# A hybrid recurrence and attention layer on one core: the second of four norm sums of a recurrence unit stands one stage of the mixer later

## The chip, the cores and the metric

The kernel runs on one core of one Trainium2 chip, as one program. The metric is the device time of one execution in microseconds (us). Before the change three runs took 2640.05, 2636.79 and 2634.97 us: a median of 2636.79 us. TensorE is called PE here, VectorE DVE, ScalarE ACT; SP issues the DMA transfers, and its queue is strictly in order.

## The reference, cut to what matters

The layer projects a normalised input (2048 tokens, 1024 channels) into nine groups of columns, runs a bidirectional gated linear recurrence over five of them and a neighbourhood attention over the other four, multiplies each branch by its gate, and projects back. The change concerns the end of the recurrence branch, for each of 8 heads:

```python
o = direction(zf_fw, lb_fw, False) + direction(zf_bw, lb_bw, True)
o = _rmsnorm(o.transpose(0, 2, 1, 3), norm_g).reshape(B, S, HG_WIDTH)
return o.astype(g_in.dtype) * jax.nn.silu(g_in)

def _rmsnorm(x, g):
    xf = x.astype(jnp.float32)
    return xf * lax.rsqrt(jnp.mean(jnp.square(xf), axis=-1, keepdims=True) + RMS_EPS) * g.astype(jnp.float32)
```

`direction` walks the tokens in chunks and carries a state from chunk to chunk, forwards once and backwards once. The mean of squares is taken over the 128 channels of a head.

## The kernel before, in words

**Phases.** The tokens are worked in two halves of 1024. A first phase holds the projections and the attention of the first half. Then comes the recurrence phase that the change touches: 16 units, one for each head and half (the loop at the end of the block below: `half, u = divmod(i, 8)`). Two more phases hold the attention of the second half and the output projection.

**What fills a unit.** `weave` interleaves two generators. The *dense* one is the projection of the next unit: groups of three 128x512 matmuls (`proj_mm`, L278; in the last unit of the phase also `vproj`, L291), which keep PE busy while the other engines work. The *mixer* is `hgrn`: for each of two groups of 512 tokens six pieces, each ended by a `yield` of a number; the pieces are called stages 0 to 5 (first group) and 6 to 11 (second group) here. The numbers, 5, 5, 3, 3, 6 and 5, say how much dense work follows each stage. So 3 units of dense work (stages 2 and 3, and 8 and 9) are the short stretches, 6 (stages 4 and 10) the long ones.

**The tail.** The outputs of a unit are finished in the next one, by a third generator, `hgrn_tail`; each stage of the mixer takes one step of it (`next(tail, None)`), 12 steps at most, before the rest of the stage's own work. In the second half (7 units with a tail in the mixer, and one tail at the end of the phase) a tail finishes four blocks of 512 tokens, and each ends in `rms_out`, with a norm sum: the two matmuls of L350 and L351, which sum the squares over the partitions.

- first output: group 1 of the second half. Stage 0 computes its backward states, stage 1 adds them on PE (L643), copies the output out of PSUM (L645) and squares it (L343 on ACT), then splits the square into a rounded part `rh` (L345 on DVE) and a rest `rl` (L347). Stage 2 holds its norm sum, the logarithm and exponential (L353, L354 on ACT), two multiplies on DVE (L355, L357) and the store to `yq` (L358).
- second output: group 0 of the second half, in the same way: L643 to L347 in stage 3, norm sum and what follows in stage 4, and with it the loads of `cl` (L661 to L663) for the third output.
- third and fourth output: the two groups of the first half, kept in DRAM since. Stage 5 multiplies the final backward state by a stored factor (`pc<-cl`, L666, two instructions on PE), adds the stored output (L667 on DVE), squares and splits; stage 6 holds the sum of the third. Stages 7 and 8 do the same for the fourth.

**What sets the order.** On PE the program order of the code is kept (`manual_schedule`). On ACT, DVE and SP a scheduler orders the instructions when the program is built, by priorities and its own estimates; on the chip each engine then runs its list strictly in order. Buffers: the tag `t` (output copy, square, rate, finished output) has 2, `cl` has 3, `rh` and `rl` have 1 each, and the PSUM tag `po`, in which `ss` and `pc` live too, has 2.

Of the kernel before, what the change touches and what calls it, by code (L numbers as in the profile page):

```python
# [21 lines left out]
HALF = 1024  # L22
# [16 lines left out]
def body(ctx: ExitStack, tc: tile.TileContext, t):  # L39
# [13 lines left out]
    @contextmanager  # L53
    def psum_phase(name, psb, pmap={}):
        with tc.tile_pool(name="p" + name, bufs=1, space=PSUM, reuse_waits="tile") as q:
            cur.update(psum=q, ps=psb, map=pmap)
            yield

    @contextmanager
    def phase(name, bufs, smap={}):  # L60
        with tc.tile_pool(name=name, bufs=1, reuse_waits="tile") as p:
            cur.update(pool=p, bufs=bufs, smap=smap)
            yield
# [24 lines left out]
    def nm(s):  # L88
        cnt[0] += 1
        return f"{s}_{cnt[0]}"  # L90

    def tl(tag, dt=F32, shape=None):
        if tag in cur["smap"]:
            tag = cur["smap"][tag]
            return sh.tile([P, 512], dt, tag=tag, name=nm(tag), bufs=SH[tag])
        return cur["pool"].tile([P, 512] if shape is None else shape, dt, tag=tag, name=nm(tag), bufs=cur["bufs"].get(tag, 1))
# [4 lines left out]
    def ps(tag="mx"):  # L101
        if tag == "pj":
            return pp.tile([P, 512], F32, tag=tag, name=nm("pj"))
        tag = cur["map"].get(tag, tag)
        return cur["psum"].tile([P, 512], F32, tag=tag, name=nm("ps"), bufs=cur["ps"][tag])
# [219 lines left out]
    def hgrn_init():  # L325
        p = cur["pool"]
        msk["mskd"] = p.tile([P, 3, 32], F32, tag="mskd", name="mskd")
        dma(msk["mskd"], t["mskd"])
        for i in range(2):
            b = p.tile([P, 2 * P], F32, tag=f"pdb{i}", name=f"pdb{i}")  # L330
            pool.memset(b, 0.0)
            pdb.append(b)
        for u in range(NHEAD):
            sfb.append(p.tile([P, P], F32, tag=f"sfb{u}", name=f"sfb{u}"))
# [3 lines left out]
        act.activation(e, e, AF.Ln, bias=1.0)  # L338
        act.activation(e, e, AF.Exp, scale=-1.0)

    def rms_out(u, g, o_sb, sg, tok):
        sq = tl("t")
        act.activation(sq, o_sb, AF.Square)  # L343
        sh_ = tl("rh", F32R)
        dve.tensor_copy(sh_, sq)  # L345
        sl_ = tl("rl", F32R)
        dve.tensor_tensor(sl_, sq, sh_, op=ALU.subtract)  # L347
        yield
        pss = ps("ss")
        pe.matmul(pss, ones, sh_, start=True, stop=False)  # L350
        pe.matmul(pss, ones, sl_, start=False, stop=True)  # L351
        r = tl("t")
        act.activation(r, pss, AF.Ln, scale=1.0 / 128.0, bias=eps_rms)  # L353
        act.activation(r, r, AF.Exp, scale=-0.5)  # L354
        dve.tensor_mul(r, r, o_sb)  # L355
        yv = tl("t")
        dve.tensor_tensor(yv, r, sg, op=ALU.mult)  # L357
        dma(yT[u][:, tok:tok + 512], yv)  # L358
# [60 lines left out]
    def hgrn(u, half, st, tail):  # L419
# [191 lines left out]
        for _ in tail:  # L611
            pass
        return hgrn_tail(u, half, sgs, ubs, decs, qibs, os_, decb_all)

    HSUM = 54

    def hgrn_tail(u, half, sgs, ubs, decs, qibs, os_, decb_all):

        R = None
        if half == 0:  # L620
            ds_ = tl("dsuf", shape=[P, 8])
            pool.memset(ds_[:, 7:8], 1.0)
            for b in range(6, -1, -1):
                dve.tensor_mul(ds_[:, b:b + 1], ds_[:, b + 1:b + 2], decb_all[:, b + 1:b + 2])
        obs = {}
        for g in (1, 0):
            po = os_[g]
            pend = []
            for b in range(3, -1, -1):
                sl = slice(b * P, (b + 1) * P)  # L630
                if R is not None:
                    pend.append((sl, R))
                if half == 0 and g == 0 and b == 0:
                    break
                rn = tl("Sb", shape=[P, P])
                if R is None:
                    dve.tensor_copy(rn, ubs[g][:, sl])
                else:
                    dve.scalar_tensor_tensor(rn, R, decs[1, g][:, b:b + 1], ubs[g][:, sl], op0=ALU.mult, op1=ALU.add)
                R = rn  # L640
            yield
            for sl, r in pend:
                pe.matmul(po[:, sl], r, qibs[1, g][:, sl], start=False, stop=True, skip_group_check=True)  # L643
            ob = tl("t")
            act.activation(ob, po, AF.Copy)  # L645
            tk = slice(g * 512, (g + 1) * 512)
            if half == 0:
                dma(op_d[u][:, tk], ob)
                dma(sg_d[u][:, tk], sgs[g])
                qb = tl("t")  # L650
                for b in range(4):
                    sl = slice(b * P, (b + 1) * P)
                    dve.tensor_scalar(qb[:, sl], qibs[1, g][:, sl], ds_[:, g * 4 + b:g * 4 + b + 1], 1.0, op0=ALU.mult, op1=ALU.mult)
                dma(qb_d[u][:, tk], qb)
            else:
                yield from rms_out(u, g, ob, sgs[g], HALF + g * 512)
        if half == 1:
            for g in range(2):
                tk = slice(g * 512, (g + 1) * 512)
                qb, o1, sg = tl("cl"), tl("cl"), tl("cl")  # L660
                dma(qb, qb_d[u][:, tk])  # L661
                dma(o1, op_d[u][:, tk])
                dma(sg, sg_d[u][:, tk])  # L663
                yield
                po = ps("pc")
                pe.matmul(po, R, qb, start=True, stop=True)  # L666
                dve.tensor_tensor(o1, po, o1, op=ALU.add)  # L667
                yield from rms_out(u, g, o1, sg, g * 512)
# [234 lines left out]
    def vstream(*pairs):  # L903
        for p2 in pairs:
            for _ in vproj(t["w_v"][p2], nv_d[p2], 1):
                yield 2.9
# [429 lines left out]
    def border_dense(dense):  # L1336
        yield from vstream(0)
        yield from dense
        yield from vstream(1)

    BTOT = NLEN + 2 * VLEN
# [8 lines left out]
    def weave(mix, dense, total, steps, last=0, ahead=0.0):  # L1350

        got, done, cum = [], [0.0], 0.0

        def upto(x):
            while done[0] < x and not got:
                try:
                    done[0] += next(dense)
                except StopIteration as e:
                    got.append(e.value)

        share = HTOT / total if last else 1.0
        upto(ahead)
        while True:
            try:
                cum += next(mix)
            except StopIteration as e:
                tail = e.value
                break
            upto(ahead + (total * share - ahead) * cum / steps)
        if last:  # L1370
            for i, _ in enumerate(tail):
                upto(total * (share + (1 - share) * (i + 1) / last))
        upto(1e9)
        return tail, got[0]

    h_alloc()
    with psum_phase("n0", NPS), tc.manual_schedule(engines={mybir.EngineType.PE}):
        with phase("st", SB_, SMS), tc.manual_schedule(engines={getattr(mybir.EngineType, e) for e in ("PE", "SP", "Activation", "DVE")}):
            raws, feed = startup()
        with phase("n0", NB0, SM0):  # L1380
            natten_init(4, 0)
            st = first_half(raws, feed)
# [7 lines left out]
    with psum_phase("h", *HPS), phase("h", HB, SMH), tc.manual_schedule(engines={mybir.EngineType.PE}):  # L1390
        hgrn_init()
        tail = iter(())
        for i in range(16):
            half, u = divmod(i, 8)
            if i < 15:
                nxt = hgrn_dense((i + 1) % 8, (i + 1) // 8, i in (6, 7), reload if i == 6 else None)
                tail, st = weave(hgrn(u, half, st, tail), nxt, HTOT, HSUM)
            else:
                raws, dense = natten_stream(0, 1)
                st0 = Prep(0, 1, raws)  # L1400
                for n in ("q", "k0", "k1", "g"):
                    st0.fetch(n)
                for c in (0, 1):
                    st0.v(c, "V0")
                weave(hgrn(u, half, st, tail), border_dense(dense), BTOT, HSUM, 9)

    wo, parts = {}, {}

# [122 lines left out]
    with psum_phase("n1", NPS), phase("n1", NB1, SM1), tc.manual_schedule(engines={mybir.EngineType.PE}):  # L1531
        natten_init(4, 1)
        st = st0
# [9 lines left out]
        for u in range(8):  # L1543
            nxt, extra = None, None
            if u < 7:
                raws, dense = natten_stream(u + 1, 1, feed, u + 1 == 7)
                total = NLEN
                if u == 0:
                    dense, total = chain(vs, dense), NLEN + 1.375 * VLEN
# [4 lines left out]
            else:  # L1554
                y_split(0, 1)
                dense, total = out_stream(list(range(NE))), NE * 16 * KUS
                extra = {0: [(wo_split, 0, 6, 7), (wo_load, 1, 2, 3)], 1: [(wo_split, 1, 0, 1), (wo_load, 1, 6, 7)], 2: [(wo_split, 1, 2, 3, 4, 5)], 3: [(wo_split, 1, 6, 7)]}
            weave(natten_woven(st, nxt, pipe, extra), dense, total, 24)
            st = nxt
# [77 lines left out]
```

## Time and profile before

| what | value |
|---|---|
| runs | 2634.97 to 2640.05 us, median 2636.79 us |
| the profiled execution's own time | 2634.39 us |
| its span, first to last instruction | 2632.5 us |
| PE busy in matmuls | 2564.7 us (97%) |
| DVE, ACT busy | 1736.9 us (66%), 1430.8 us (54%) |
| mean granted clock of PE | 0.992 |
| stretch with the seven second-half tails in the mixer | 1180 to 1702 us |
| one such unit, from first norm sum to first norm sum (1191.56 to 1267.23 us) | 75.7 us |

Times in the profile are counted from the first instruction. A row of the timeline gives the start, the length, the engine, the line of the kernel, the operation, `out<-in` by tile names, the shapes, and how many instructions are merged in the row; in square brackets stands how long the engine had sat idle, and who ended that. A busy PE is one with a matmul in flight: consecutive 128x512 matmuls start 0.23 us apart but last 0.4 us each, so a small wait shows as a longer distance between starts before it shows as idle time.

### The profile page before, as it was taken

How to read it: one execution, taken by the hardware profiler on the slowest of the kernel's cores; microseconds unless marked ns; L12 is line 12 of the kernel's file. 1: busy time of each engine (PE TensorE's matmuls, PEld its weight loads, DVE VectorE, ACT ScalarE, POOL GpSimd, SP SyncE). 2: the span in 40 equal slices, each digit the busy share in tenths (PEclk: the TensorE clock that was granted, in tenths of full speed). 3: DMA queues.
4: the chain of work that ended last, by engine and by line, in shares of the span. 5: the costliest groups of instructions: out<-in, count | busy, mean ns of one | idle time of the engine just before them, and what ended most of it. 6: DMA issues, size and time to landing. Idle time of an engine off the chain costs nothing.

```text
span 2632.5 us, 45805 instructions
## 1 busy us (share of the span) xinstructions
PE 2564.7 (97%) x17140; PEld 2150.0 (82%) x17140; DVE 1736.9 (66%) x4354; ACT 1430.8 (54%) x2856; POOL 108.7 (4%) x143
## 2 busy tenths in 40 slices
PE   6999999989999999999999999999999998999998
PEld 5888888878888888888888888888888887788887
DVE  7444545377777778877787777555777778548443
ACT  4534444366666666666666666454677777431110
POOL 0000000000000000000000000000000000042221
PEclk9999999999999999999999999999999999999999
DMA  7466454212111126212221222344455556443331
GB/s 271 140 212 143 132 174 152 94 46 69 65 65 58 64 73 220 84 46 77 77 65 57 72 74 73 107 120 146 126 139 140 142 142 173 125 154 128 96 96 57
DMA packets 225631, 295.87 MB, mean 112 GB/s; under 512 B 28807, under 2 KB 117511, under 8 KB 224263
## 3 DMA queue, kind: packets, MB, share of 16 engines
q1 hardware_dynamic: 225407, 292.93, 36.4%
q8 instruction: 135, 2.21, 0.4%
q14 instruction: 89, 0.73, 0.1%
HBM read 217.65 MB, written 66.99 MB: 108 GB/s over the span
## 4 chain that ended last, share of the span: by engine, by line
PE 73%; DVE 3%; ACT 2%; DMA 1%; issue 0%; DVEq 0%; ACTq 0%
PE pj L278 39%; PE ps L1466 4%; PE ps L1467 4%; PE ps L1468 4%; PE pj L291 3%; PE ps L1098 3%; PE ps L1076 2%; PE ps L478 2%; PE ps L470 1%; PE ps L545 1%; PE ps L1027 1%; PE ps L569 1%; PE ps L517 1%; PE ps L571 1%; PE ps L643 1%; DMA yq<-t 1%
## 5 line engine op out<-in xcount | busy, mean ns | idle before, releaser
L278 PE MATMUL pj<-h,wh 128*128 128x512 f32 x4000 | 1272.7, 399 | 4.2 <-ACT wh L815 1.9
L278 PEld LDWEIGHTS pj<-h,wh 128*128 128x128 f32 x4000 | 724.9, 188 | 156.3 <-issue 13.9
L278 PE MATMUL pj<-h,wl 128*128 128x512 f32 x2000 | 783.5, 392 | 0.0
L278 PEld LDWEIGHTS pj<-h,wl 128*128 128x128 f32 x2000 | 375.4, 188 | 82.9 <-DVE wl L791 0.4
L1048 ACT ACTIVATE pbuf<-pbuf,mx 128x480 f32<-128x480 f32 (+5 forms) x256 | 152.4, 597 | 114.0 <-DVE mx L1043 113.2
L291 PE MATMUL pj<-wh,h 128*128 128x256 f32 x1024 | 198.8, 289 | 4.1 <-ACT vt L297 3.8
L1043 DVE CUSTOM_DVE_ANT_1 pbuf<-ps,bias 128x480 f32<-128x480 f32 (+5 forms) x256 | 129.1, 540 | 105.1 <-PE ps L1034 47.1
L291 PEld LDWEIGHTS pj<-wh,h 128*128 128x128 f32 x1024 | 165.5, 194 | 7.9 <-ACT vt L297 4.5
L268 ACT ACTIVATE wh<-wr 128x512 fp32r<-128x512 f32 x192 | 120.2, 626 | 81.6 <-PE pj L278 72.3
L269 DVE TENSOR_TENSOR wl<-wr,wh 128x512 fp32r<-128x512 f32 x192 | 131.6, 685 | 46.7 <-ACT wh L268 45.8
L291 PE MATMUL pj<-wl,h 128*128 128x256 f32 x512 | 146.1, 285 | 0.0
L1082 ACT ACTIVATE pt<-ps 120x384 f32<-120x384 f32 (+3 forms) x128 | 65.2, 509 | 117.8 <-PE ps L1076 117.5
L464 DVE TENSOR_TENSOR de<-e,de 128x512 f32<-128x512 f32 x64 | 44.3, 692 | 117.6 <-ACT de L463 117.6
L1080 DVE COPY pt<-ps 120x384 f32<-120x384 f32 (+3 forms) x128 | 75.0, 586 | 65.3 <-PE ps L1076 64.1
L1076 PE MATMUL ps<-ident,pbuf 128*128 128x128 f32 (+2 forms) x832 | 113.3, 274 | 1.7 <-DVE pbuf L1053 1.3
L1076 PEld LDWEIGHTS ps<-ident,pbuf 128*128 128x128 f32 (+2 forms) x832 | 97.2, 137 | 19.3 <-ACT pbuf L1048 1.7
L764 ACT ACTIVATE e<-pj 128x512 f32<-128x512 f32 x98 | 58.3, 595 | 86.6 <-PE pj L278 79.6
L1442 ACT ACTIVATE yh<-yr 128x512 fp32r<-128x512 f32 x52 | 32.7, 628 | 132.4 <-PE ps L1467 115.2
L1053 DVE TENSOR_SCALAR pbuf<-pbuf,mx 128x480 f32<-128x480 f32 (+5 forms) x256 | 101.2, 413 | 3.9
L1515 DVE TENSOR_TENSOR vt<-ps,gt 128x512 f32<-128x512 f32 x24 | 16.5, 691 | 130.6 <-PE ps L1468 130.6
L291 PEld LDWEIGHTS pj<-wl,h 128*128 128x128 f32 x512 | 99.5, 194 | 1.4 <-issue 0.5
L445 DVE TENSOR_TENSOR_SCAN c<-c,g 128x128 f32<-128x128 f32 x256 | 88.4, 405 | 10.7 <-ACT c L435 10.7
(274 smaller groups left out, 4684.9 us busy)
## 6 DMA issues: line engine op xcount, KB each, us to landing
wr<-in_w_in SPq DMA_DIRECT2D x276, 256.0 KB
yr<-yq SPq DMA_DIRECT2D x64, 256.0 KB
bias<-tint SPq DMA_DIRECT2D x24, 480.0 KB
x<-in_x SPq DMA_DIRECT2D x32, 256.0 KB
ada<-in_ada_m SPq DMA_DIRECT2D x8, 1024.0 KB
wr<-in_w_v SPq DMA_DIRECT2D x32, 256.0 KB
nv<-vt SPq DMA_DIRECT2D x32, 256.0 KB
hs<-s SPq DMA_DIRECT2D x32, 256.0 KB
```

Source lines behind the costliest of these rows:

```text
L268: act.activation(hi, raw, AF.Copy)
L269: dve.tensor_tensor(lo, raw, hi, op=ALU.subtract)
L278: pe.matmul(pz, a, b, start=(k == 0 and n == 0), stop=(k == KT - 1 and n == 2))
L291: pe.matmul(pzs[tp][:, i * 256:(i + 1) * 256], a, b, start=(k == 0 and n == 0 and i == 0), stop=(k == KT - 1 and n == 2), skip_group_check ...
L445: dve.tensor_tensor_scan(c[:, sl], c[:, sl], L[:, sl], 0.0, op0=ALU.add, op1=ALU.subtract)
L1043: return dve.tensor_tensor_reduce(s[:, 0:nk].rearrange("p (r c) -> p r c", c=kw), sc[:, 0:nk].rearrange("p (r c) -> p r c", c=kw), bt[:, 0 ...
L1048: act.activation(s[:, 0:nk], s[:, 0:nk], AF.Exp, scale=-1.0, bias=mx[:, 0:1], accum_out=mx[:, 1:2])
L1053: dve.tensor_scalar(s[:, 0:nk], s[:, 0:nk], mx[:, 2:3], 1.0, op0=ALU.mult, op1=ALU.mult)
L1076: pe.transpose(ptp[0:cw, c * P:(c + 1) * P], s[:, c * cw:(c + 1) * cw], ident)
L1466: pe.matmul(pz, yh[:, kk], wh, start=first, stop=False)
L1467: pe.matmul(pz, yh[:, kk], wl, start=False, stop=False)
L1468: pe.matmul(pz, yl[:, kk], wh, start=False, stop=last)
```

## The change

The generator `rms_out` gets a flag; with it, it yields once more between the split of the square and the norm sum. The second output (group 0 of the second half) passes the flag. So its norm sum moves from stage 4 to stage 5, and everything behind it in the tail moves one stage: the third output's product from stage 5 to 6 and its sum from 6 to 7, the fourth's from 7 and 8 to 8 and 9. The tail now takes 10 steps of the 12. The last tail, which runs against the value projection, is told 10 steps in place of 9; there PE's order comes out as before. No instruction is added or removed.

```diff
-    def rms_out(u, g, o_sb, sg, tok):
+    def rms_out(u, g, o_sb, sg, tok, rest=False):
...
         dve.tensor_tensor(sl_, sq, sh_, op=ALU.subtract)
         yield
+        if rest:
+            yield
         pss = ps("ss")
...
-                yield from rms_out(u, g, ob, sgs[g], HALF + g * 512)
+                yield from rms_out(u, g, ob, sgs[g], HALF + g * 512, g == 0)
...
-                weave(hgrn(u, half, st, tail), border_dense(dense), BTOT, HSUM, 9)
+                weave(hgrn(u, half, st, tail), border_dense(dense), BTOT, HSUM, 10)
```

In the changed kernel the lines behind the new yield are two higher: the sums of L350 and L351 are L352 and L353, the product of L666 is L668, and so on.

Place 1: PE in stages 4 and 5 of the first unit concerned (numbers behind the names are buffers; between the rows left out stand dense matmuls). Before:

```order
L470 MATMUL ps_12610<-ident,de_12540 128x128 x4
...
L350 MATMUL ps_12631<-rh_12593,ones 128x512
L351 MATMUL ps_12631<-rl_12595,ones 128x512
L478 MATMUL ps_12647<-v_12390,ke_12615 128x128 x4
...
L666 MATMUL ps_12752<-cl_12641,Sb_12524 128x512
L545 MATMUL ps_12761<-x_12687,x_12688 64x64 x8
```

The same place on PE now:

```order
L472 MATMUL ps_12610<-ident,de_12540 128x128 x4
...
L480 MATMUL ps_12631<-v_12390,ke_12615 128x128 x4
...
L352 MATMUL ps_12736<-rh_12593,ones 128x512
L353 MATMUL ps_12736<-rl_12595,ones 128x512
L547 MATMUL ps_12752<-x_12671,x_12672 64x64 x8
```

The second sum (`rh_12593`, `rl_12595`) has left its place behind 12 dense matmuls and ahead of the state updates (L478, now L480), and stands where the third output's product stood, 27 dense matmuls further on.

Place 2: stages 8 and 9 of the same unit, PE first and then ACT. Before, on PE, from stage 7 on:

```order
L666 MATMUL ps_12881<-cl_12840,Sb_12524 128x512
...
L350 MATMUL ps_12948<-rh_12886,ones 128x512
L351 MATMUL ps_12948<-rl_12888,ones 128x512
L470 MATMUL ps_12958<-ident,de_12908 128x128 x4
...
L478 MATMUL ps_13005<-v_12828,ke_12963 128x128 x4
```

The same place on PE now:

```order
L668 MATMUL ps_12939<-cl_12875,Sb_12524 128x512
L472 MATMUL ps_12948<-ident,de_12899 128x128 x4
...
L352 MATMUL ps_12995<-rh_12944,ones 128x512
L353 MATMUL ps_12995<-rl_12946,ones 128x512
L480 MATMUL ps_13005<-v_12819,ke_12953 128x128 x4
```

On ACT before, there:

```order
L343 ACTIVATE t_12884<-cl_12841 128x512
L353 ACTIVATE t_12951<-ps_12948,eps_rms 128x512
L472 ACTIVATE ke_12963<-ps_12958 128x512
L463 ACTIVATE de_13310<-c_13233 128x128 x4
L354 ACTIVATE t_12951<-t_12951 128x512
```

And on ACT now:

```order
L474 ACTIVATE ke_12953<-ps_12948 128x512
L465 ACTIVATE de_13310<-c_13233 128x128 x4
L343 ACTIVATE t_12942<-cl_12876 128x512
L387 ACTIVATE vt_12980<-pj_12917 128x512
L268 ACTIVATE wh_13244<-wr_13242 128x512
L355 ACTIVATE t_12998<-ps_12995,eps_rms 128x512
```

The fourth output's product (L668) now opens stage 8, and its sum (`rh_12944`, `rl_12946`) opens stage 9, behind four transposes (L472) and 15 dense matmuls; on ACT its square (L343) stands behind the copy of the transposes and four exponentials.

Place 3: DVE in the seventh unit (the last of the phase) between the second output's split and the mask of the scores (`pm`, which PE waits for in stage 6). Before:

```order
L347 TENSOR_TENSOR rl_17656<-t_17652,rh_17654 128x512
L269 TENSOR_TENSOR wl_17878<-wr_17875,wh_17877 128x512
L355 TENSOR_TENSOR t_17705<-t_17705,t_17650 128x512
L555 COPY_PREDICATED pdb_5315<-mskd,ps_17725 128x128
L357 TENSOR_TENSOR t_17709<-t_17705,sg_16463 128x512
...
L667 TENSOR_TENSOR cl_17713<-ps_17834,cl_17713 128x512
...
L345 CAST rh_17839<-t_17837 128x512
L558 TENSOR_TENSOR pm_17860<-pdb_5315 32x4x32 x4
```

The same place now:

```order
L347 TENSOR_TENSOR rl_17656<-t_17652,rh_17654 128x512
L269 TENSOR_TENSOR wl_17869<-wr_17866,wh_17868 128x512
L557 COPY_PREDICATED pdb_5315<-mskd,ps_17709 128x128
...
L560 TENSOR_TENSOR pm_17851<-pdb_5315 32x4x32 x4
L357 TENSOR_TENSOR t_17821<-t_17821,t_17650 128x512
```

The second output's two multiplies, the third output's addition (L667) and its rounding (L345) no longer stand ahead of the mask.

On SP the second output's store moves behind two loads of weights, and two further loads of weights move ahead of the fourth output's `cl<-op`; the count of transfers is the same.

## The prediction

> **What bounds the kernel now.** I read the page first, then PE's waits in the stretch of the change, then PE's rows around the norm sums. The page has the span and PE's share:
>
> ```profile
> span 2632.5 us, 45805 instructions
> PE 2564.7 (97%) x17140; PEld 2150.0 (82%) x17140; DVE 1736.9 (66%) x4354; ACT 1430.8 (54%) x2856; POOL 108.7 (4%) x143
> ```
>
> PE is the bound, so only what PE waits for, or runs slowly, can be won. PE's waits from 1180 to 1640 us, the first six of the seven units concerned (in total, times, longest):
>
> ```profile
> PE ps L350 <- DVE rh L345: 2.6, 6, 0.6
> PE ps L351 <- DVE rl L347: 1.4, 6, 0.2
> ```
>
> Six waits each: one of four norm sums per unit. The rows of PE in the first unit say which, and show a sum that does not wait (1231.45); then stand the sums of the sixth unit and of the seventh:
>
> ```profile
> 1200.68 0.39 PE L278 MATMUL pj<-h,wl 128*128 128x512 f32 x1
> 1201.58 0.49 PE L350 MATMUL ps<-rh,ones 128*128 128x512 f32 x1 [0.51 <-DVE rh L345]
> 1202.31 0.50 PE L351 MATMUL ps<-rl,ones 128*128 128x512 f32 x1 [0.23 <-DVE rl L347]
> 1231.22 0.40 PE L278 MATMUL pj<-h,wl 128*128 128x512 f32 x1
> 1231.45 0.40 PE L350 MATMUL ps<-rh,ones 128*128 128x512 f32 x1
> 1231.92 0.60 PE L470 MATMUL ps<-ident,de 128*128 128x128 f32 x4
> 1579.47 0.49 PE L350 MATMUL ps<-rh,ones 128*128 128x512 f32 x1 [0.41 <-DVE rh L345]
> 1580.20 0.50 PE L351 MATMUL ps<-rl,ones 128*128 128x512 f32 x1 [0.23 <-DVE rl L347]
> 1655.11 0.28 PE L291 MATMUL pj<-wh,h 128*128 128x256 f32 x1
> 1658.73 0.49 PE L350 MATMUL ps<-rh,ones 128*128 128x512 f32 x1 [3.35 <-DVE rh L345]
> 1659.46 0.50 PE L351 MATMUL ps<-rl,ones 128*128 128x512 f32 x1 [0.23 <-DVE rl L347]
> ```
>
> It is the second sum, the one the change moves. Start to start it costs more than its idle time: 0.90 us from 1200.68 to 1201.58 where 0.23 is the rule (1231.22 to 1231.45), and 0.73 to L351 where an unhindered pair takes 0.47 together. That is 0.67 + 0.49 = 1.16 us in the first unit and 0.08 to 0.10 less in the sixth, by its idle time; over the six, whose idle times before L350 are 0.43 on average (2.6 / 6) against 0.51 here, 1.08 each, or 6.5. In the seventh it is 3.62 - 0.12 = 3.5, and 0.5: 4.0.
>
> The long wait has a second price. The same work, state updates and diagonal blocks, in the first unit and behind the long wait (busy times of PE, PEld, DVE, ACT, POOL with counts, PEclk, DMA share, GB/s):
>
> ```profile
> 1202.64:1204.46 1.82, 1.82 (x73) 1.65 (x71) 0.00 (x0) 1.82 (x4) 0.00 (x0) 1.00 0.00 0
> 1659.80:1662.83 3.03, 3.03 (x73) 2.74 (x71) 0.90 (x2) 1.91 (x3) 0.00 (x0) 0.54 0.29 87
> 1662.83:1664.50 1.67, 1.67 (x19) 1.67 (x12) 1.53 (x4) 0.00 (x0) 0.00 (x0) 0.81 0.05 10
> ```
>
> At a granted clock of 0.54 it took 1.21 us more; the next 1.67 us, at 0.81, lost 0.19 x 1.67 = 0.3. Together 1.5. The Trainium skill ("TensorE: Matmul & The Clock Gate", Part 1) says that PE falls to half its clock after an idle window of about 3.4 us and comes back after about as long a busy one. The trace agrees: 3.35 us idle, then 0.54. By the page alone the price would be half of 3.4, an estimate of 1.7 us, and the total below 0.2 us better.
>
> Why the second sum waits, from the chain that ended last, taken in this stretch:
>
> ```profile
> 1197.12 3.23 DMA yq<-t
> 1200.43 0.64 ACT t L343
> 1201.10 0.44 DVE rh L345
> 1201.56 0.70 DVE rl L347
> 1202.31 0.50 PE ps L351
> ```
>
> The first output's store holds one of the two `t` buffers, the square of the second output needs it, and the stretch from stage 3 to stage 4 is short. In the seventh unit the same store held ACT until 1657.59.
>
> **The second sum, removed from stage 4.** It goes behind 27 more dense matmuls and the updates: over 6 us, against operands ready at most 0.7 us too late before. It waits no more: 6.5 us from six units, 4.0 + 1.5 = 5.5 from the seventh.
>
> **The third output** keeps five units of dense work between product and sum (stages 6 to 7), 21 matmuls of 0.23. The cover is 4.8 us for an addition (0.69 in a row below), a square and a split (0.64, 0.44 and 0.70 above), 2.5 us. I cost it at nothing, and 2.3 us are to spare for what DVE does between.
>
> **The fourth output, the new short stretch.** Product and sum are now in stages 8 and 9, with 15 dense matmuls between, where the second output had 12. Rows for the handoffs there (PE, ACT, DVE):
>
> ```profile
> 1235.82 1.06 PE L478 MATMUL ps<-v,ke 128*128 128x128 f32 x8
> 1236.71 0.60 PE L470 MATMUL ps<-ident,de 128*128 128x128 f32 x4
> 1237.41 0.60 ACT L472 ACTIVATE ke<-ps 128x512 f32<-128x512 f32 x1 [0.99 <-PE ps L470]
> 1237.90 1.27 ACT L463 ACTIVATE de<-c 128x128 f32<-128x128 f32 x4
> 1239.20 0.69 DVE L464 TENSOR_TENSOR de<-e,de 128x512 f32<-128x512 f32 x1 [0.66 <-ACT de L463]
> ```
>
> Count from the start of the four transposes. PE reaches the sum after 3.90 us (1231.92 to 1235.82: transposes and 15 matmuls), the second matmul of the pair at 4.13. ACT copies the transposes from 0.70 on, runs four exponentials from 1.19, and only then squares; DVE multiplies at 2.49 and rounds (`rh`) at about 3.1, splits (`rl`) 0.46 later at 3.56, and PE takes `rl` 0.75 after that (1201.56 to 1202.31): 4.31. `rh` is in time by 0.3 (0.48 from 1201.10 to 1201.58); `rl` is 0.18 late. So 0.2 us per unit, 1.1 in six. Bounds: nothing, if DVE takes `rh` before the multiply; the old 1.16, if the stretch behaves like the one it replaces. I take 0.2, since order and handoffs are those of these rows. In the seventh unit the exponentials are not there, and I take nothing.
>
> What waits behind: DVE now puts the fourth output's two multiplies between the four state updates of stage 9 (L489), which free the buffer for the products of stage 10. By the same count the last ends some 0.2 us before PE needs it. I cost it at nothing, at most 0.2 a unit.
>
> **The loads and stores.** The load of `op` for the fourth output waits on SP for the third output's multiply, as now (SP's waits, 1186 to 1640 us); then how long such a load takes, at its one wait in the last tail, and how long the multiply comes behind the sum:
>
> ```profile
> SPq L662 <- DVE t L355: 110.4, 12, 11.0
> 1739.63 0.33 SPq L662 DMA_DIRECT2D cl<-op  x1
> 1742.83 0.69 DVE L667 TENSOR_TENSOR cl<-ps,cl 128x512 f32<-128x512 f32 x1 [1.08 <-DMA cl<-op]
> 1220.79 0.40 PE L351 MATMUL ps<-rl,ones 128*128 128x512 f32 x1
> 1222.88 0.69 DVE L355 TENSOR_TENSOR t<-t,cl 128x512 f32<-128x512 f32 x1 [0.57 <-ACT t L354]
> ```
>
> Multiply 2.1 behind the sum, done 0.7 later, load 3.2 (1739.63 to 1742.83): 6.0 us after the third sum. The fourth product ends 21 matmuls (4.8), the pair's rest and itself later, about as late. As the square must queue behind four exponentials anyway, the load has 1.5 us to spare. The second output's store now stands behind two loads of weights; if its buffer came late, the third output's 2.3 us to spare would take it. Both at nothing.
>
> **The seventh unit gets a new wait.** There ACT still sits until the store lands, and PE, no longer held at stage 4, arrives early at the masked scores of stage 6:
>
> ```profile
> 1657.59 0.63 ACT L343 ACTIVATE t<-t 128x512 f32<-128x512 f32 x1 [2.96 <-DMA yq<-t]
> 1659.32 0.68 DVE L269 TENSOR_TENSOR wl<-wr,wh 128x512 fp32r<-128x512 f32 x1
> 1662.97 0.30 DVE L555 COPY_PREDICATED pdb<-mskd,ps 128x128 f32<-128x128 uint32 x1 [0.84 <-PE ps L517]
> 1670.02 0.69 DVE L667 TENSOR_TENSOR cl<-ps,cl 128x512 f32<-128x512 f32 x1 [0.74 <-PE ps L666]
> 1674.25 1.17 DVE L558 TENSOR_TENSOR pm<-pdb 32x128 f32<-32x128 f32 x4
> 1675.56 0.46 PE L569 MATMUL ps<-pm,v 128*128 128x128 f32 x2 [0.19 <-DVE pm L558]
> ```
>
> DVE can start L555 at 1659.92 in place of 1662.97 (3.05 earlier) and has three instructions and a wait less before `pm`: one multiply 0.6, L667 with its wait 1.35, the rounding 0.33. So `pm` comes 5.3 us earlier. PE alone would come 6.8 earlier: 4.0 + 1.5, some 0.3 for the wait it has there now (0.19 idle and a late start), 0.6 since the pair of sums no longer stands ahead of the updates, and 0.4 since the pair of 0.47 now stands where a product stood, which is longer (the chain, first unit):
>
> ```profile
> 1210.86 0.86 PE ps L666 x2
> ```
>
> The last two are only work put off. PE waits 1.5 us, and the unit gives 5.5 + 0.3 - 1.5 = 4.3. The wait may be nothing, if ACT and DVE catch up, or 3 us, if DVE cannot start L555 earlier at all and saves only the three instructions; I keep the count, since each instruction ahead of L555 has its row.
>
> **Sum.** 6.5 - 1.1 + 4.3 = 9.7 us less. Later work is PE's own row of matmuls and keeps it. The profiled execution took 2634.39 us, 1.9 over its span and 2.4 under the median; from the median, 2636.79 - 9.7 = 2627.1 us. 0.2%, about what a measurement of this kernel tells from no change, is 5.3 us.
>
> **Rivals.**
> - The wait only changes places: the fourth sum waits 1.08 as the second did. For it: the same short stretch, and a square behind five ACT instructions. Against: 15 matmuls in place of 12, 0.7 us more, and no store in the chain. Gain 4.3: 2632.5 us. Chance 0.10.
> - PE is held anyway: DVE's `pm`, or the third sum, is late in all units as `pm` is in the seventh. For it: ACT's list is still blocked by the store. Against: six units block it for tenths only. No gain: 2636.8 us. Chance 0.05.
> - Slower: the load of `op` comes late. Two loads of weights now stand right ahead of it. It decides from 1.5 us on; past it, every us is 7 us for the kernel. Landing 4.5 us later than counted gives 7 x 3.0 - 9.7 = 11 us more: 2648 us. Against: 3.2 us per load in the row above. Chance 0.09.
> - All is won, no new wait at the fourth sum nor at `pm`: 9.7 + 1.1 + 1.5 = 12.3: 2624.5 us. Chance 0.13.
> - The forecast, 2627.1 us: 0.63.
>
> The range, 2622.5 to 2634.0, holds the forecast, the full gain and the changed place, with 2 us for the scatter of runs at the ends. Faster by over 0.2% (below 2631.5): 0.63 + 0.13 = 0.76; within: 0.15; slower: 0.09.
>
> **What would show it.** In the changed profile the second sum (L352, L353, at stage 5) has no wait on `rh`; the wait on `rl` (L353) remains, at stage 9, with about 0.2 us; the seventh unit shows a wait of PE on `pm` of 1 to 2 us and a granted clock near 1.00 after stage 4. A wait on `rh` near 0.5 at stage 9, or DVE waiting for the DMA of `cl<-op`, would make me wrong.

## The result, and the profile after

Six runs of the changed kernel took 2623.76 to 2628.38 us, median 2625.66; the kernel before, beside it, 2632.80 to 2640.05, median 2635.36. The ratio is 0.9965, with a 95% interval of 0.9956 to 0.9975: 9.7 us less. The prediction was 2627.1 us and 9.7 us less, so the time was right to 1.5 us and the difference to a tenth. That it was right to a tenth is luck, since the interval of the ratio reaches from 6.6 to 11.6 us less. How far the steps behind it were right is another question; the traces answer it first.

The span and PE's share, from the page of the changed kernel; its profiled execution took 2628.06 us, one of the two longest of the six:

```profile
span 2626.3 us, 45803 instructions
PE 2562.5 (98%) x17140; PEld 2149.1 (82%) x17140; DVE 1738.8 (66%) x4354; ACT 1434.5 (55%) x2856; POOL 108.7 (4%) x143
```

PE's waits from 1180 to 1640 us: the list is empty, where the kernel before had twelve. PE's rows of the norm sums in the first unit, with the first instruction behind the fourth sum, and the first sum of the units that follow (start, length, engine, line, operation):

```profile
1191.73 0.40 PE L352 MATMUL ps<-rh,ones 128*128 128x512 f32 x1
...
1209.15 0.40 PE L352 MATMUL ps<-rh,ones 128*128 128x512 f32 x1
1209.39 0.40 PE L353 MATMUL ps<-rl,ones 128*128 128x512 f32 x1
...
1234.34 0.40 PE L352 MATMUL ps<-rh,ones 128*128 128x512 f32 x1
1234.69 0.50 PE L353 MATMUL ps<-rl,ones 128*128 128x512 f32 x1
1235.02 1.05 PE L480 MATMUL ps<-v,ke 128*128 128x128 f32 x8
...
1266.43 0.40 PE L352 MATMUL ps<-rh,ones 128*128 128x512 f32 x1
...
1641.14 0.39 PE L352 MATMUL ps<-rh,ones 128*128 128x512 f32 x1
...
1712.04 0.39 PE L352 MATMUL ps<-rh,ones 128*128 128x512 f32 x1
```

The second sum (1209.15) follows its neighbours at the pace of a sum that waits for nothing: 0.24 us to its second half. The fourth sum (1234.34) is the one that pays now. Its second half starts 0.35 us behind it instead of 0.24, and the state updates 0.33 behind that: 0.2 us per unit, too little to show as idle time. A unit takes 74.70 us (1191.73 to 1266.43). The same three marks in the kernel before, first sum of the first unit, of the seventh, and of the last tail:

```profile
1191.56 0.40 PE L350 MATMUL ps<-rh,ones 128*128 128x512 f32 x1
...
1646.37 0.39 PE L350 MATMUL ps<-rh,ones 128*128 128x512 f32 x1
...
1722.15 0.39 PE L350 MATMUL ps<-rh,ones 128*128 128x512 f32 x1
```

Six units took 454.81 us and take 449.41: 5.4 less, 0.90 each. The seventh took 75.78 and takes 70.90: 4.9 less. Its rows after the change (PE), and the granted clock of the stretch that ran at 0.54 before:

```profile
1649.99 1.05 PE L480 MATMUL ps<-v,ke 128*128 128x128 f32 x8
...
1657.66 0.39 PE L352 MATMUL ps<-rh,ones 128*128 128x512 f32 x1
1657.89 0.40 PE L353 MATMUL ps<-rl,ones 128*128 128x512 f32 x1
...
1664.57 0.46 PE L571 MATMUL ps<-pm,v 128*128 128x128 f32 x2 [0.90 <-DVE pm L560]
```

```profile
1649.90:1653.00 3.10, 3.10 (x85) 2.94 (x84) 0.55 (x2) 0.98 (x2) 0.00 (x0) 1.00 0.33 120
```

The second sum waits for nothing, the clock stays at 1.00, and PE meets `pm` 0.90 us early.

So the recurrence gave 10.3 us. The two profiled executions differ by only 6.3 (2634.39 to 2628.06): this one lost 4 us again behind it, most of it at one place in the attention of the second half. Its rows, ACT and PE:

```profile
2200.98 0.63 ACT L1428 ACTIVATE wo<-vt 128x512 fp32r<-128x512 f32 x1 [3.17 <-DMA vt<-in_w_out]
...
2207.04 1.50 PE L1078 MATMUL ps<-ident,pbuf 128*120 128x128 f32 x6 [3.41 <-DVE pbuf L1055]
```

ACT stood 3.17 us before a load of output weights, the exponentials of the attention stood behind that in its queue, and PE waited 3.41 us for them and then took 1.50 us for six transposes, at a granted clock of 0.50 that lasted until 2209.80 us. In the kernel before, this place reads:

```profile
2213.73 0.84 PE L1076 MATMUL ps<-ident,pbuf 128*120 128x128 f32 x6 [1.30 <-DVE pbuf L1053]
```

That is 2.1 us of wait and 0.7 us of transposes more. Whether this belongs to the change is the question of one run below.

### The profile page after: what moved, and what is told of

Read it like the earlier page. It is cut to its first block, busy times and chain, and to the rows that moved or that the text cites. A ratio compares the mean times of both kernels' runs of the same rounds, so it can differ in the third digit from the quotient of the medians.

```text
span 2626.3 us, 45803 instructions
## 1 busy us (share of the span) xinstructions
PE 2562.5 (98%) x17140; PEld 2149.1 (82%) x17140; DVE 1738.8 (66%) x4354; ACT 1434.5 (55%) x2856; POOL 108.7 (4%) x143
## 4 chain that ended last, share of the span: by engine, by line
PE 72%; DVE 2%; DMA 2%; ACT 2%; issue 0%; DVEq 0%; SPq 0%; ACTq 0%
PE pj L278 39%; PE ps L1468 4%; PE ps L1469 4%; PE ps L1470 4%; PE pj L291 2%; PE ps L1100 2%; PE ps L1078 2%; PE ps L480 2%; PE ps L472 2%; PE ps L547 1%; PE ps L1029 1%; PE ps L571 1%; PE ps L573 1%; PE ps L519 1%; PE ps L645 1%; DMA bias<-tint 1%
## 5 line engine op out<-in xcount | busy, mean ns | idle before, releaser
L1078 PEld LDWEIGHTS ps<-ident,pbuf 128*128 128x128 f32 (+2 forms) x832 | 97.3, 137 | 22.8 <-ACT pbuf L1050 3.8
```

What stands on the lines that cost most here:

```text
L1078: pe.transpose(ptp[0:cw, c * P:(c + 1) * P], s[:, c * cw:(c + 1) * cw], ident)
```

## The experiments

The first study took the change apart and tried two other ways to the same end. Each kernel ran in several rounds beside the kernel before (27 runs of it, median 2635.58 us).

**Six units without the seventh.**

```diff
-                yield from rms_out(u, g, ob, sgs[g], HALF + g * 512, g == 0)
+                yield from rms_out(u, g, ob, sgs[g], HALF + g * 512, g == 0 and u < 6)
...
-                weave(hgrn(u, half, st, tail), border_dense(dense), BTOT, HSUM, 10)
+                weave(hgrn(u, half, st, tail), border_dense(dense), BTOT, HSUM, 9)
```

> The extra step in six of the seven tails only (heads 0 to 5, 1180 to 1640 us); the seventh and the last tail as before. Theory (each wait of PE before the second sum is paid one for one): 0.90 us per unit from first sum to first sum (75.60 to 74.70), 5.4 us in all, and the seventh unit keeps its wait of about 3.4 us on `rh` and its clock of about 0.54. Rival (the gain of the seventh unit came from the units ahead of it, by another alignment of stores and loads): the seventh unit is also shorter, and the gain is near 9.7.

Measured: 2630.40 us, ratio 0.9981 (0.9972 to 0.9990): 5.2 us less, as the theory has it. The six units take 449.4 us. The seventh waits a little less than before, 2.68 us, and the clock falls all the same (PE's row, and the window from that row on):

```profile
1654.42 0.80 PE L352 MATMUL ps<-rh,ones 128*128 128x512 f32 x1 [2.68 <-DVE rh L345]
```

```profile
1654.42:1655.74 1.32, 1.32 (x3) 0.79 (x3) 1.27 (x2) 0.00 (x1) 0.00 (x0) 0.51 0.00 0
```

**The seventh unit alone.**

```diff
-                yield from rms_out(u, g, ob, sgs[g], HALF + g * 512, g == 0)
+                yield from rms_out(u, g, ob, sgs[g], HALF + g * 512, g == 0 and u == 6)
...
-                weave(hgrn(u, half, st, tail), border_dense(dense), BTOT, HSUM, 10)
+                weave(hgrn(u, half, st, tail), border_dense(dense), BTOT, HSUM, 9)
```

> The extra step in the seventh tail only (head 6). Theory: the six units stay at 75.6 us each, with PE's wait of 0.4 to 0.5 us on `rh` at stage 4; the seventh loses its wait and its low clock and gives 4.3 by the prediction, 4.9 as the changed kernel's trace reads. Rival (the gain of that unit hangs on the six ahead of it): nothing, 0 to 1 us.

Measured: 2630.58 us, ratio 0.9981 (0.9972 to 0.9990): 5.0 us less. PE's waits from 1180 to 1640 us show the six units as they were (total, times, longest):

```profile
PE ps L352 <- DVE rh L345: 2.1, 6, 0.6
PE ps L353 <- DVE rl L347: 1.4, 6, 0.2
```

The seventh unit takes 70.50 us, 5.3 less than before. The two halves of the change are independent, and together (10.2) they are the whole, within the intervals. The last tail, which has the extra step in neither of them, gives nothing: from its first sum to its fourth it takes 22.6 to 22.8 us before the change, after it and in these two kernels.

**A third buffer instead of a later stage**, on the kernel before (the end of `HB`, the list of buffer counts of the recurrence phase):

```diff
-"t": 2, "cl": 3, "rh": 1, "rl": 1}
+"t": 3, "cl": 3, "rh": 1, "rl": 1}
```

> The kernel before with 3 buffers of `t` instead of 2 and no change of stages. Theory (the first output's store holds the buffer that the square of the second needs, and that makes the second sum late): the second output's copy and square run some 2 us earlier in six units and 5 us earlier in the seventh, the second sum waits for nothing at stage 4 though its stretch is as short as before, no sum at stage 9 comes late for `rl`, and the gain is 6.5 + 4.3 to 5.8, about 11 us. Rival (the short stretch alone makes it late: 12 matmuls are too few for a copy, a square and a split): the wait on `rh` stays above 0.3 us in the six units, and the gain is at most 5 us, from the seventh.

Measured: 2624.48 us, ratio 0.9955 (0.9943 to 0.9968): 11.1 us less. The rows around the second output in the first unit (ACT copies and squares, DVE rounds, PE sums):

```profile
1198.59 0.60 ACT L645 ACTIVATE t<-ps 128x512 f32<-128x512 f32 x1 [0.92 <-PE ps L643]
...
1199.22 0.63 ACT L343 ACTIVATE t<-t 128x512 f32<-128x512 f32 x1
...
1200.13 0.42 DVE L345 CAST rh<-t 128x512 fp32r<-128x512 f32 x1
...
1202.50 0.40 PE L350 MATMUL ps<-rh,ones 128*128 128x512 f32 x1
...
1202.73 0.39 PE L351 MATMUL ps<-rl,ones 128*128 128x512 f32 x1
```

The same two instructions of ACT in the kernel before:

```profile
1197.19 0.60 ACT L645 ACTIVATE t<-ps 128x512 f32<-128x512 f32 x1 [1.10 <-DVE t L357]
...
1200.43 0.63 ACT L343 ACTIVATE t<-t 128x512 f32<-128x512 f32 x1 [0.28 <-DMA yq<-t]
```

There the square came 3.24 us behind the start of the copy: with no buffer free until the store had landed, the build had put a copy and four exponentials between them, and the square still waited 0.28 us for the store. Here it follows 0.63 us behind, and `rh` is ready 2 us before the sum. The first output's store was issued only 0.5 us before this square (1198.71 us) and takes about 3.2, so the square no longer waits for it. The stretch between product and sum is as short as it was. So its shortness was not the cause by itself; the missing buffer was, by the wait and by the order of ACT's list, which the build made with this buffer count as its only difference. A unit takes 74.43 us, 0.27 less than with the change, and the seventh 71.27, with a wait of 1.34 us on `pm`.

**A longer stretch, the stages as before:**

```diff
             forward_states(g, updates(ke0, v))
             ke1 = turned(de1, "ke")
-            yield 3
+            yield 4 if half and g == 0 else 3
...
-            yield 6
+            yield 5 if half and g == 0 else 6
```

> The kernel before, and in the second half's units one unit of dense work (6 matmuls, 1.4 us) is moved from behind stage 4 to behind stage 3, so that the second sum stands 18 in place of 12 matmuls behind the product; the order of the stages is as before. Theory (only the missing cover of about 1.2 us counts): the six waits go (6.5 us), the seventh keeps about 2.6 of its 4.0 and stays below the idle time after which the clock fell, so about 1.4 + 1.5 more: 8 to 9 us less, if nothing behind stage 4 becomes late. Rival (the six matmuls were needed behind stage 4, for the level factors `x` or the loads of `cl`): a new wait there of up to 1.4 us a unit, and a gain of 0 to 3 us.

Measured: 2638.21 us, ratio 1.0011 (1.0002 to 1.0019): 2.6 us more, within 0.2% but on the other side, and neither expectation had a loss. The six waits of the second sum went, as the theory says. In their place stands one at the third sum, on `rl`, of 1.24 us in the first unit. PE and DVE there:

```profile
1222.19 0.48 PE L350 MATMUL ps<-rh,ones 128*128 128x512 f32 x1
...
1222.52 0.40 DVE L536 TENSOR_TENSOR x<-x,e 128x256 f32<-128x256 f32 x1
...
1222.83 0.42 DVE L537 TENSOR_TENSOR x<-x,e 128x256 f32<-128x256 f32 x1
...
1223.17 0.69 DVE L347 TENSOR_TENSOR rl<-t,rh 128x512 fp32r<-128x512 f32 x1
...
1223.91 0.50 PE L351 MATMUL ps<-rl,ones 128*128 128x512 f32 x1 [1.24 <-DVE rl L347]
```

And DVE in the kernel before, around the same split:

```profile
1219.14 0.67 DVE L347 TENSOR_TENSOR rl<-t,rh 128x512 fp32r<-128x512 f32 x1
...
1220.37 0.40 DVE L536 TENSOR_TENSOR x<-x,e 128x256 f32<-128x256 f32 x1
```

With six matmuls fewer behind stage 4, DVE's list, which the build orders anew, has the split behind all four scans (L445) and two of the level factors' multiplies, where it stood behind two scans. The third sum's pair then takes 1.72 us from start to start, where it took 0.32. A unit gains about 1.1 and loses 1.4 and comes out at 75.97 us. The six matmuls stand ahead of the third output's product; from the product to the sum it is 9.77 us in both kernels. Two things came together: DVE begins the third output's addition 2.12 us behind the start of the product, where it was 1.06, and it has the split later in its list. How much each is worth is not separated. The rival was right that taking the six matmuls from behind stage 4 makes a wait, and wrong about which operand comes late. The seventh unit also missed its expectation: the wait on `rh` stayed at 3.01 us, not 2.6, the granted clock fell to 0.50 behind it, and the unit takes 76.4 us, 0.6 more than before.

The second study looked at what was left open (the kernel before, 15 runs, median 2634.80 us).

**The changed kernel once more.**

> The changed kernel once more, for one place: in its first profiled execution PE waited 3.4 us for `pbuf` (L1055) at 2207 us, in the attention of the second half, where the kernel before and the four kernels of the first study waited 1.3 to 1.6 us. Theory (that was one execution's late load, not a part of the change): the wait is 1.3 to 1.6 us here, and the span is about 2 us shorter. Rival (the shorter recurrence sets the loads of this place against others, and the wait belongs to the change): 3.4 us again. In both cases the recurrence reads as before: 74.70 us per unit, no wait of PE before the second sum, about 0.9 us on `pm` in the seventh unit.

Measured: 2624.60 us, ratio 0.9958 (0.9946 to 0.9971), 10.2 us less. The late place, ACT and PE:

```profile
2198.08 0.63 ACT L1428 ACTIVATE wo<-vt 128x512 fp32r<-128x512 f32 x1 [0.46 <-DMA vt<-in_w_out]
...
2204.73 0.84 PE L1078 MATMUL ps<-ident,pbuf 128*120 128x128 f32 x6 [1.30 <-DVE pbuf L1055]
```

The wait is 1.30 us, as before the change, and the span is 2622.8 us, 9.7 under the 2632.5 of the kernel before. So the 3.4 us were a late load of one execution. The six units take 449.4 us again, the seventh 71.42 (70.90 in the first trace), with 1.05 us on `pm` and a new wait of 0.27 us ahead of it, for a copy of ACT (`vt`, L297).

**The change and the third buffer together**, in `HB` as above, on the changed kernel.

```diff
-"t": 2, "cl": 3, "rh": 1, "rl": 1}
+"t": 3, "cl": 3, "rh": 1, "rl": 1}
```

> The changed kernel with 3 buffers of `t`. Theory (the extra step and the third buffer take away the same lateness of the same sum): together they give no more than the third buffer alone, 10 to 12 us under the kernel before; the sum of the fourth output still comes 0.1 us late for `rl`; the wait on `pm` in the seventh unit falls from 0.9 us towards nothing, since ACT no longer stands before the store. Rival (they take away different things): the gains add to about 20 us.

Measured: 2625.62 us, ratio 0.9958 (0.9945 to 0.9970): 9.2 us less, no more than either. They remove the same lateness. The six units read as with the change alone (449.4 us). In the seventh, PE's row at `pm` has no wait left, and the unit takes 69.90 us:

```profile
1665.86 0.46 PE L571 MATMUL ps<-pm,v 128*128 128x128 f32 x2
```

So the 0.9 us on `pm` hung on the buffer too: in the changed kernel ACT still stands before the first output's store, with the rest of its list behind it. The buffer alone, without the extra step, had left 1.34 us there.

**The extra step at the first output instead of the second.**

```diff
-                yield from rms_out(u, g, ob, sgs[g], HALF + g * 512, g == 0)
+                yield from rms_out(u, g, ob, sgs[g], HALF + g * 512, g == 1)
```

> The extra step stands at the first output in place of the second: its norm sum in stage 3 instead of 2, the second output's product in stage 4 and its sum in stage 5, the rest as in the changed kernel. Theory (the second sum needs the stretch between its product and itself to cover the first output's store): by the rows of the kernel before, the first sum then stands at about 1196 us, its store lands 8.9 us later, 1204.9, and the second sum's operands are ready at 1207, with PE there at 1210.7: no wait, and the same gain of 9 to 11 us, though the store is later by a stage. Rival (the store holds the square wherever it stands, and lands later with its own sum): the wait of 0.5 us per unit stays, and the gain is below 3 us.

Measured: 2630.05 us, ratio 0.9981 (0.9972 to 0.9990): 4.7 us less, half of what was expected. The seven units did as the theory says: 74.71 us each, no wait at a sum, and 70.32 the seventh, with 0.75 us on `pm`. What failed is that the flag also acts on the last tail, and there the stretches are shorter still. PE's row of the second sum of the last tail, and the clock behind it:

```profile
1723.74 0.72 PE L352 MATMUL ps<-rh,ones 128*128 128x512 f32 x1 [2.44 <-DVE rh L345]
```

```profile
1724.46:1725.13 0.67, 0.59 (x3) 0.50 (x2) 0.02 (x1) 0.00 (x0) 0.00 (x0) 0.50 0.00 0
```

The same edit without the last tail (`g == 1 and u < 7`, and 9 in place of 10 in the last `weave`) tested that:

> As first_rests, but without the extra step in the last tail, which then is that of the kernel before (9 steps). In first_rests the seven units in the mixer took as long as in the changed kernel (74.71 us, and 70.3 the seventh), and the last tail had a new wait of 2.44 us on its second sum. Theory (that wait and the low clock behind it are what first_rests lost against the changed kernel): without it the gain is 9 to 11 us. Rival (the seven units are not what sets the time there): it stays near 5 us.

Measured: 2624.63 us, ratio 0.9959 (0.9946 to 0.9971) against 2635.92: 11.3 us less. The loss was the last tail's. And within the intervals it does not matter which of the two outputs rests, as long as the second sum has a long stretch ahead of it.

**A second extra step, for the fourth output.**

```diff
-                yield from rms_out(u, g, o1, sg, g * 512)
+                yield from rms_out(u, g, o1, sg, g * 512, g == 1)
...
-                weave(hgrn(u, half, st, tail), border_dense(dense), BTOT, HSUM, 10)
+                weave(hgrn(u, half, st, tail), border_dense(dense), BTOT, HSUM, 11)
```

> The changed kernel with a second extra step, before the fourth output's sum, which moves from stage 9 to stage 10 (11 steps of the 12). Theory (`rl` comes 0.1 us late there because the stretch is short): the two matmuls of the fourth sum start 0.23 us apart instead of 0.34, and a unit takes 74.6 instead of 74.7 us; 0.6 us in all, below what the times can tell. Rival (the lateness follows the sum): 0.34 at the new place, or a wait on a later piece of the tail.

One execution, 2624.00 us; a difference of a microsecond is not to be read from it, but the trace is plain. The fourth sum of the first unit, at its new place, and what follows it:

```profile
1238.27 0.40 PE L352 MATMUL ps<-rh,ones 128*128 128x512 f32 x1
1238.50 0.39 PE L353 MATMUL ps<-rl,ones 128*128 128x512 f32 x1
1238.73 1.05 PE L480 MATMUL ps<-v,ke 128*128 128x128 f32 x8
```

0.23 and 0.23, in place of 0.35 and 0.33, and each unit takes 74.51 us: 0.19 less. In the last tail the extra step again made a wait, of 2.31 us.

**The best of the parts:** three buffers of `t`, and the extra step in the seventh tail alone.

```diff
-                yield from rms_out(u, g, ob, sgs[g], HALF + g * 512, g == 0)
+                yield from rms_out(u, g, ob, sgs[g], HALF + g * 512, g == 0 and u == 6)
...
-"t": 2, "cl": 3, "rh": 1, "rl": 1}
+"t": 3, "cl": 3, "rh": 1, "rl": 1}
...
-                weave(hgrn(u, half, st, tail), border_dense(dense), BTOT, HSUM, 10)
+                weave(hgrn(u, half, st, tail), border_dense(dense), BTOT, HSUM, 9)
```

> A candidate from the parts that gave most: 3 buffers of `t`, and the extra step in the seventh tail alone. Theory (the parts act unit by unit): six units as in third_t, 74.43 us, the seventh as in changed_third_t, 69.9 us with no wait on `pm`; from the first sum to the last tail's first sum 517.7 us, where third_t has 519.1 and the changed kernel 520.3 to 520.8; the gain is 12 to 13 us. Rival (with the six units unchanged the seventh again meets `pm` late): 519.1, as third_t, and a gain of 11.

Measured: 2621.72 us, ratio 0.9952 (0.9938 to 0.9965) against 2635.92: 14.2 us less. The interval overlaps that of the change (0.9956 to 0.9975), so by the times alone it is not shown to be faster than the changed kernel. The trace has it 2.6 to 3.1 us shorter in the recurrence: 517.70 us from the first sum to the last tail's first, against 520.31 and 520.83. That is six units of third_t (447.8) and the seventh at 69.89.

## Why the prediction was right, step by step

The length of the units, from the first sum of one to the first sum of the next, carries the comparison, since the first five units agree to about a hundredth of a microsecond within each kernel whose second sum does not wait, and from one execution of the changed kernel to the other:

| kernel | six units, us | the seventh, us |
|---|---|---|
| before | 454.8 | 75.8 |
| changed, two executions | 449.4, 449.4 | 70.9, 71.4 |
| six units only | 449.4 | 74.8 |
| seventh only | 454.4 | 70.5 |
| third buffer | 447.8 | 71.3 |
| change and third buffer | 449.4 | 69.9 |
| longer stretch | 457.0 | 76.4 |

- **The second sum's wait, 1.08 us in six units, and the fourth sum's 0.2 against it.** Net 0.90 us a unit was forecast, and 0.90 was measured (454.81 to 449.41 over six). The part on `rl` was 0.18 by count and is about 0.2 by the rows at 1234.34 to 1235.02; with that sum moved off, the unit fell by 0.19. The forecast sign, that `rl` and not `rh` would be late there, held. Only the place where it would show did not: the prediction named a wait of about 0.2 us on `rl` in the list of waits, and the list is empty, since the lateness hides inside a running matmul. That the net agrees to the hundredth is luck. The count of 1.16 us in the first unit leaves out that the state updates, too, start late behind the pair (0.33 us, 1202.31 to 1202.64, where 0.23 is free), and by the rows it is 1.26. At the fourth sum the same tenth is inside the measured 0.2. The rows would have given 1.18 - 0.21 = 0.97; the 0.07 between that and the measured 0.90 is not traced.
- **The seventh unit, 4.3 us.** Measured 4.9 and 4.4, and 5.3 in the kernel with the seventh step alone (5.0 by its time). The clock stayed at 1.00, as forecast. The mis-sized term is the new wait on `pm`: 1.5 by count, 0.90 and 1.05 measured, and 0.50 with the seventh step alone. The second of the two executions also has the 0.27 us on `vt`, which the count does not know. The matmul on `pm` came 5.8 us earlier against the first sum (1646.37 to 1675.56 before, 1641.14 to 1664.57 now), where the count had 5.3 for `pm`. That the wait hung on ACT and the store was right in part: on top of the change the third buffer took it to nothing, but alone it leaves 1.34 us. There the third output's addition still stands ahead of the mask in DVE's list, as in the kernel before, so the buffer alone is not the whole of it; the prediction counted both.
- **The cause of the wait: the store holds a buffer, and the stretch is short.** The prediction named both. The third buffer shows that the first is enough to mend: with a buffer free the short stretch is long enough. What the prediction had not said is that the missing buffer also shaped ACT's order, which is most of the 2.8 us by which the square came earlier, counted from the first sum (1200.43 - 1191.56 = 8.87 before, 1199.22 - 1193.15 = 6.07 with the third buffer).
- **The third output's 2.3 us to spare.** It was costed at nothing, and no wait of PE stands at the third sum. That its cover depends on when DVE gets to the addition and the split is what the longer stretch showed: with six matmuls fewer ahead of the product and another order on DVE, the sum came 1.4 us late in each unit.
- **The load of `op`.** It was costed at nothing too, and it cost nothing, but with less room than the 1.5 us that the prediction had to spare. "DVE waiting for the DMA of `cl<-op`" was named as a sign that the prediction is wrong, and this sign is there: before the fourth output's addition DVE sat idle for 2.98 to 3.90 us in each of the six units, and in four of them the load came last. Before the change it did not wait there. The fifth unit after the change (DVE, ACT), and its addition before:

```profile
1530.78 0.69 DVE L669 TENSOR_TENSOR cl<-ps,cl 128x512 f32<-128x512 f32 x1 [3.90 <-DMA cl<-op]
...
1531.55 0.62 ACT L343 ACTIVATE t<-cl 128x512 f32<-128x512 f32 x1
```

```profile
1530.30 0.69 DVE L667 TENSOR_TENSOR cl<-ps,cl 128x512 f32<-128x512 f32 x1
```

The addition ended 0.08 us before ACT was through with its four exponentials and came to the square; in the other five units 0.4 to 1.0 us were left. So the slower rival, a load late enough to delay the sum, did not come about, and the fourth sum reads alike in all six units. The sign was badly chosen: idle time of DVE at this place costs nothing as long as the square has to queue behind the exponentials.

- **"The wait only changes places"** gave 1.08 us at the fourth sum; it was 0.2. **"All is won"** would have been 2624.5 us; other edits did get these parts, a step more for the fourth sum and a third buffer for `pm`, but this change does not.
- **"Later work is PE's own row of matmuls and keeps it."** Over the medians it does. In one execution about 3 us of it went to a late load of weights 490 us later, which the second execution did not show. The step holds here, and leaves out that a single profile can hide a third of such a gain.
- **From which time the sum is made.** The prediction subtracted from 2636.79; the median of the six runs beside the changed kernel was 2635.36. That is the 1.5 us by which the time was off, while the difference was right. (At its upper end the range leaves 1.5 us for the scatter of runs, not the 2 us that it names.)

## What to carry to other kernels

When an engine waits a little in every unit, follow its operand back to the buffer it needs, not only to the instruction before it: here a store held a buffer, and a third buffer won as much as a later stage. Before moving work to lengthen one stretch, count what the neighbouring stretch covers, and look at the order that the build then makes: here six matmuls taken from behind one stage, with a new order on DVE, moved the wait to the next sum and made it longer. A sign that would show a prediction wrong should lie on the path that sets the time: an engine that waits where nothing hangs on it decides nothing. And read a gain of a few microseconds from marks inside the trace, such as the start of the same matmul in each unit, since the whole span of one execution can differ by several microseconds for reasons elsewhere.

## What the runs showed of the hardware that was not expected

The prediction had one fall of PE's clock to go by, behind 3.35 us of idle time, and the expectation for the longer stretch counted on 2.6 us being too short. The runs say otherwise: after 2.68 us idle (six units only) the granted clock was 0.51, after 2.44 us (the last tail of first_rests) 0.50. In the same way the kernel with the fourth step, behind its 2.31 us (PE's row, and the window behind it):

```profile
1724.75 0.69 PE L352 MATMUL ps<-rh,ones 128*128 128x512 f32 x1 [2.31 <-DVE rh L345]
```

```profile
1726.07:1728.30 2.23, 2.23 (x12) 2.23 (x11) 0.61 (x1) 1.32 (x2) 0.00 (x0) 0.50 0.00 0
```

After 1.30 us, in the second execution of the changed kernel, the clock stayed (the window behind that wait):

```profile
2204.73:2206.50 1.77, 1.77 (x11) 1.60 (x12) 1.74 (x7) 1.77 (x6) 0.00 (x0) 1.00 0.80 233
```

So in these kernels 2.3 us of idle time or more were enough wherever they occurred in the stretch of the change, and 1.3 us were not. In between, the length alone does not decide. Every execution has the same wait of 1.90 us at about 278 us, for a weight tile (`wh`). Behind it the clock fell in seven of the twelve profiled executions and stayed at 1.00 in five. One of each, six units only and then the kernel before (PE's row, and the 2.5 us from it on):

```profile
278.78 1.15 PE L278 MATMUL pj<-h,wh 128*128 128x512 f32 x2 [1.90 <-ACT wh L817]
278.78:281.28 2.50, 2.50 (x6) 1.93 (x7) 1.87 (x3) 0.98 (x2) 0.00 (x0) 0.52 0.61 203
```

```profile
277.96 0.73 PE L278 MATMUL pj<-h,wh 128*128 128x512 f32 x2 [1.90 <-ACT wh L815]
277.96:280.46 2.50, 2.50 (x10) 1.78 (x11) 1.88 (x3) 0.99 (x2) 0.00 (x0) 1.00 0.64 204
```

What decides between them is open. The Trainium skill ("TensorE: Matmul & The Clock Gate", Part 1) puts the fall at an idle window of about 3.4 us; the measurement decides here, and shorter idle times were enough. A wait of 2.3 us already cost more than its own length.

The granted clock of a window can also be a mixture. The 0.54 and the 0.81 behind the long wait of the kernel before are parts of one stretch at 0.50, with 1.00 ahead of it (from 1658.73 us, where the wait ends) and 1.00 behind it:

```profile
1660.06:1663.47 3.41, 3.41 (x75) 3.12 (x74) 1.19 (x3) 1.91 (x3) 0.00 (x0) 0.50 0.25 77
```

A third one: the profiled executions reach the first unit concerned at quite different times, with the same source ahead of it. The first sum stood at 1191.56 us before the change, at 1195.23 in the kernel with the seventh step alone and at 1191.28 in the last kernel. That scatter of 4 us lies ahead of the stretch that the change touches. A part of it goes with the clock behind the wait of 1.90 us: from the end of this wait to the first sum it is 913.6 to 913.8 us in the five executions whose clock stayed, and 914.5 to 915.1 us in five of those whose clock fell (in the other two the first sum stands at another stage). The scatter is about as large as that between runs (2623.76 to 2628.38), though the runs without a profile can't be traced, so that the one makes the other is not shown.
